# HGRN2 feature tile by feature tile from step 0.2 on, with TensorE's queue of the first stage in text order

## The chip, the cores and the metric

The kernel runs on one core of one Trainium2 chip, in one launch. The metric is the device time of one execution in microseconds (us). Five engines matter, each with a queue of its own that it works off from the front: TensorE for matmuls (PE in the profile; PEld is its weight load), VectorE (DVE), ScalarE (ACT), GpSimd (POOL) and SyncE (SP), which issues DMAs.

## What is computed

A decoder trunk of two layers over 1,024 positions and 1,024 features, in float32. Each layer projects the normed input once and splits the columns among four groups of 256 features: latent attention (A), forgetting attention (B), HGRN2 (C) and S5 (D). Their outputs go through an output projection into the residual, then come a gated MLP with a short convolution and a gated embedding. The change touches the groups C and D and the projection that feeds them:

```python
def hgrn2_group(q, f_logit, i_in, lb):              # group C, chunks of 64 positions
    ...
    def chunk_step(state, inp):
        q_c, k_c, v_c, lf_c = inp
        bcum = jnp.cumsum(lf_c, axis=2)
        decay = jnp.exp(jnp.where(causal[:, :, None], bcum[:, :, :, None, :] - bcum[:, :, None, :, :], -jnp.inf))
        scores = jnp.einsum('bhtk,bhsk,bhtsk->bhts', q_c, k_c, decay)
        o = jnp.einsum('bhts,bhsv->bhtv', scores, v_c) + jnp.einsum('bhtk,bhkv->bhtv', q_c * jnp.exp(bcum), state)
        ...                                          # the state goes on to the next chunk
def s5_group(u, ...):                                # group D: a complex diagonal scan, then
    zact = jax.nn.gelu(y)
    out = zact * jax.nn.sigmoid(zact @ w_glu + b_glu)
```

## The kernel before, in words

Tiles hold 128 features by 512 positions: a group of 256 features has two feature tiles (ft 0 and 1), the sequence two halves (n 0 and 1). A float32 product is three matmuls of rounded parts: pj (L738 to L740) for projections with features on partitions, 12 matmuls of 128x512 per weave step; ptk (L726 to L728) for those with positions on partitions.

The first stage of a layer is woven from generators by weave() (L683), which always advances the one with the lowest scheduled fraction, from the table T (L42):

- in_proj(), 68 steps from 0 to 1, the input projection: hq of ft 0 and the values v, then the mark "h0" (step 12, fraction 0.18); z and hq of ft 1, then "h1" (step 20, fraction 0.29); the misc tile, the attention's fq, fk and fv, HGRN2's output gates hg, and cq and ckv for attention A.
- s5(), from 0.1 to 0.7: for each ft its matrices and its core (sin L579; a chain of DVE instructions L585 to L609 on tiles s5z; ys L619 and L622; yf L635); then for all four tiles a GELU (L657 to L662, back and forth between ACT and DVE, to zh and zl), and the GLU: matmuls gl from zh and zl, and on ACT and DVE a sigmoid (L128 to L136, L676) for each of four gl tiles; then the norm (sq, ss L798, xn).
- hgrn(), 66 steps from 0.35 to 0.92: four units hgrn_unit, one for each (ft, n); a unit of n=1 takes over the state of n=0. A unit computes its gates (ACT and DVE, L217 to L237, to hk and hb), then kh (L267 to L269), transposes it on PE (khT, L292) and multiplies by v into pu (L301, the state); then comes a triangle of scores in seven levels: per level DVE L279, ACT L280 and L281, DVE L282 and twice L286 (qz), on PE four matmuls psc (L327), and on DVE L333 (into sc), each qz prepared one level ahead; at the end the diagonal (L337, L338) and poh (L351, L353).
- early(), in layer 0 only, from 0 to 0.2: constants.

Before, hgrn() waits for "h1", and then runs the units of both ft of n=0 in alternation, and after them those of n=1. The order in which each engine's queue holds this work is not that of the text: a scheduler of the framework orders all queues by its own estimates of durations and of what is ready. So a pj tile may stand ahead of a gl whose input comes late.

Around it: a first part of the projection (uf, z of ft 0) stands ahead of the weave; attention and the output projection (first instruction ob, L726), the MLP and the embedding follow.

Of the kernel before, what the change touches and what calls it, by code (L numbers as in the profile page):

```python
# [38 lines left out]

T = dict(early=(0, 0.2), s5=((0.1, 0.7), (0.1, 0.7)), hgrn=((0.35, 0.92), (0.35, 0.92)), cd=((0.05, 0.85), (0.05, 0.85)), prep=((0.3, 1), (0.3, 1)), b=(0, 1), a=(0.9, 0.95), pre=(7, 9, 11, 13), vals=(5, 6), ahead=3, plv=4, mx=0, pw=1, rt=2, sc=2, rp=6, dl=4, qk=(4, 4), up=5)  # L42


class Kern:
# [210 lines left out]
def hgrn_unit(K, layer, ft, n, z, q, v, lbc, st, y):  # L256
# [55 lines left out]
    for li in range(len(LEVELS) + 1):  # L312
        if li < len(LEVELS):
            g, qz = ahead
        if li == T['qk'][layer]:
            qk = K.h(name="qk")
# [42 lines left out]
HGRN_STEPS = 7 + len(LEVELS) + 1  # L359
# [283 lines left out]
S5_STEPS = 7 + 7  # L643
# [37 lines left out]
GLU_STEPS = 5  # L681


def weave(*gens):

    live = [[g, n, 0, span] for g, n, *span in gens]
    while live:
        e = min(live, key=lambda e: e[2] / e[1] if not e[3] else e[3][0] + (e[3][1] - e[3][0]) * e[2] / e[1])
        e[2] += 1
        try:  # L690
            next(e[0])
        except StopIteration:
            live.remove(e)
# [138 lines left out]
RMS_STEPS = 6  # L832
# [7 lines left out]
def proj(K, srcs, xs, evacs, m=P, banks=None, ws=None):  # L840

    ws = ws or [wload(K, s, len(xs) * m, hi_act=True, eng=K.nc.vector) for s in srcs]
    for n in range(2):
        for w, evac, bank in zip(ws, evacs, banks or [K.pd] * 3):
            ps = bank("pj")
            for _ in mm3_steps(K, ps[0:m, :], [(rows(*w, k, m), x[n]) for k, x in enumerate(xs)]):
                yield
            evac(n, ps[0:m, :])
            yield
# [19 lines left out]
class Head:  # L869
# [67 lines left out]

    def out(self, ahead=T['ahead']):

# [22 lines left out]
        for qh, kt in [(0, kt) for kt in range(4)] + [(1, kt) for kt in range(8)]:  # L962
# [11 lines left out]
            nc.scalar.activation(pr[:, 0:n], ps[:, 0:n], AF.Exp)  # L974
            K.lo(V if T['plv'] and kt % T['plv'] == T['plv'] - 1 else nc.gpsimd, pl[:, 0:n], pr[:, 0:n], ph[:, 0:n])
            pend.append((qh, kt, n, ph, pl))
# [8 lines left out]
def attention(heads):  # L985
# [13 lines left out]
    for i in range(len(heads)):  # L999
        nxt, pre = get(i + 2), iter(())  # L1000
        mx, vals = (b.max(), b.values()) if b else (iter(()), iter(()))
        for step, _ in enumerate(a.out()):
            for _ in range(2 if step % 2 or step < T['mx'] else 1):
                next(mx, None)
            if step == 6 and nxt:
# [3 lines left out]
                pre = nxt.prep()  # L1009
            if step in T['pre']:  # L1010
                next(pre, None)
            if step in T['vals']:
                next(vals, None)
# [9 lines left out]
def fox_cum(K, misc, bf):  # L1023


    nc = K.nc
    V = nc.vector
    r = slice(64, 68)
    prev = 0.0
    for n in range(2):  # L1030
        m, x, a = misc[n], K.h(name="fx"), K.h(name="fa")
        V.tensor_scalar(x[r], m[r], bf[r, 0:1], None, op0=ALU.add)
        nc.scalar.activation(a[r], x[r], AF.Abs)
        nc.scalar.activation(a[r], a[r], AF.Exp, scale=-1.0)
        nc.scalar.activation(a[r], a[r], AF.Ln, bias=1.0)
        V.scalar_tensor_tensor(x[r], x[r], 0.0, a[r], op0=ALU.min, op1=ALU.subtract)
        V.tensor_tensor_scan(a[r], K.ones[r, 0:1].to_broadcast([4, HS]), x[r], prev, op0=ALU.mult, op1=ALU.add)
        prev = a[r, HS - 1:HS]
        nc.gpsimd.memset(m[64:96, :], 0.0)
        nc.gpsimd.memset(m[96:102, :], 1.0)  # L1040
        V.tensor_scalar(m[r].bitcast(F32R), a[r], -1.0, None, op0=ALU.mult)
        V.scalar_tensor_tensor(m[96:100].bitcast(F32R), a[r], -1.0, m[r], op0=ALU.mult, op1=ALU.subtract)
# [409 lines left out]
def body(ctx, tc, xT, pT, pos, invf, sgn, vecs, prms, dsk, bfs, w_fm, w_misc, w_tm, w_uq, w_ukv, w_glu,  # L1452
         w_outb, w_up, w_down, w_pg, w_ple, out):
    nc = tc.nc
    K = Kern(tc, ctx)
# [45 lines left out]
    steps, lbc = [], K.const([P, 6], F32, "lbc")  # L1501
    ready = {}

    def early():

        for l in range(DEPTH):
            head = K.sm([P, 24], name="s5h", tag="s5h", bufs=2)
            nc.scalar.dma_start(head, prms[l][:, 0:24])
            steps.append(s5_steps(K, head))
            yield  # L1510
        rope_tables(K, pos, cst, tabs)
        K.exp_ln()
        hgrn_lb(K, vec[0][:, V_LB:V_LB + 4], lbc)
        ready["steps"] = True
        yield
        for _ in hgrn_consts(K):
            yield
        ready["consts"] = True
# [3 lines left out]
    for l in range(DEPTH):  # L1522
# [5 lines left out]
        z, hq, hv, hg, fq, fk, fv, misc, cq = ([] for _ in range(9))  # L1528

        def put(dst, name, m=P):  # L1530
            t = K.two(name=name)
            dst.append(t)
            return lambda n, ps: V.tensor_tensor(t[n][0:m, :], ps, r1[n], op=ALU.mult) if m == P else \
                V.tensor_tensor(t[n][0:m, :], ps, r1[n][0:m, :], op=ALU.mult)

        def fm(i, dst, name):
            return proj(K, [w_fm[l, i]], xs, [put(dst, name)])


        rt = K.sm([P, 8], name="rt", tag="rt", bufs=2)  # L1540

        def tokmaj(i, vt):
            def ev(gr, ps):
                t = K.h(name="v").rearrange("p (c f) -> p c f", f=256)
                vt.append(t)
                for j in range(2):
                    nc.scalar.activation(t[:, j, :], ps[:, j * 256:(j + 1) * 256], AF.Copy,
                                         scale=rt[:, 2 * gr + j:2 * gr + j + 1])

            return proj_tok(K, [w_tm[l, i, j] for j in range(2)], xs, ev)  # L1550
# [17 lines left out]
        def in_proj():  # L1568
            yield from fm(2, hq, "hq")
            yield from tokmaj(0, hv)  # L1570
            ready["h0"] = True
            yield from fm(1, z, "z")
            yield from fm(3, hq, "hq")
            ready["h1"] = True
            yield from proj(K, [w_misc[l]], xs, [put(misc, "misc", 68)], m=68)
            fox_cum(K, misc[0], bf)
            yield from fm(4, fq, "fq")
            yield from fm(6, fk, "fk")
            yield from tokmaj(2, fv)
            yield from fm(5, fq, "fq")  # L1580
            yield from fm(7, fk, "fk")
            for i in range(2):
                g = K.two(name="hg")

                def ev(n, ps):
                    t = K.h(name="sg")
                    V.tensor_tensor(g[n], ps, r1[n], op=ALU.mult)
                    K.sigmoid(g[n], g[n], t)

                yield from proj(K, [w_fm[l, 11 + i]], xs, [ev])  # L1590
                hg.append(g)
            ready["gates"] = True
            for i in range(2):
                yield from fm(8 + i, cq, "cq")
            yield from fm(10, cq, "ckv")

        IN_STEPS = 4 * 13 + 2 * 8
        yc, yd = [K.two(name="yc") for _ in range(2)], []
        yb, ya = ([K.two(name=n) for _ in range(2)] for n in ("yb", "ya"))
        h, ycs, yds, res, heads = [], [], [], {}, []  # L1600

        def s5():
            while "steps" not in ready:
                yield
            pr, yl = s5_params(K, prm, steps[l]), []
            for ft in range(2):
                r = {}
                yield from s5_mats(K, pr, ft, dk, r)
                yield from s5_core(K, r, uf[ft], yl)
            yield from s5_glu(K, yl, w_glu[l], vc[:, V_BGLU:V_BGLU + 2], yd)  # L1610
            yield from rms_steps(K, yd, gain(3), yds)

        def hgrn():
            st = [K.h(name="st") for _ in range(2)]
            while "h1" not in ready or "consts" not in ready:
                yield
            for n in range(2):
                u = [hgrn_unit(K, l, ft, n, z[ft][n], hq[ft][n], hv, lbc, st[ft], yc[ft]) for ft in range(2)]
                for _ in range(HGRN_STEPS):
                    for g in u:  # L1620
                        next(g, None)
                        yield
            while "gates" not in ready:
                yield
            yield from rms_steps(K, yc, gain(2), ycs, gates=hg)
# [17 lines left out]
            return get  # L1643

        pre = [(early(), 12, *T['early'])] if l == 0 else []
        weave(*pre, (s5(), 2 * S5_STEPS + GLU_STEPS + RMS_STEPS, *T['s5'][l]), (hgrn(), 4 * HGRN_STEPS + RMS_STEPS, *T['hgrn'][l]), (in_proj(), IN_STEPS, 0, 1))

        ready["fox"] = True

# [105 lines left out]
        xs, rp = nm.xs, nm.r  # L1755
# [6 lines left out]
        ws, pend, pw = {}, None, {}  # L1762
# [7 lines left out]
        for i, u in enumerate(units + [None]):  # L1770
# [3 lines left out]
            if pend:  # L1774
                n, m, c, v, t = pend
                V.scalar_tensor_tensor(t[:, c], v[:, c], 0.0, t[:, c], op0=ALU.min, op1=ALU.subtract)
                nc.scalar.activation(v[:, c], t[:, c], AF.Exp)
            if u:
                n, m, c = u
# [20 lines left out]
            if pend:  # L1800
                n, m, c, v, t = pend
# [101 lines left out]
```

## Time and profile before

| | us |
|---|---|
| median of 3 runs (lowest, highest) | 3041.83 (3039.55, 3045.96) |
| the profiled execution, its own time | 3032.95 |
| its span in the trace | 3031.2 |
| first stage, layer 0: from the first pk of S5 to the first ob | 88 to 425 |
| first stage, layer 1: the same | 1595 to 1906 |
| busy share of the span: PE, DVE, ACT, POOL | 93%, 73%, 47%, 35% |

The profile gives each instruction of each engine with its start and duration, and for a gap ahead of it the instruction that ended the gap. PEclk is the clock that TensorE was granted, as a share of its full 2.4 GHz: 1.00 is 2.4 GHz and 0.50 is 1.2 GHz. PE time in a window is the time in which some matmul was under way, so at the lower clock the same matmul counts for longer.

### The profile page before, as it was taken

The numbers are of one execution on the slowest core, as the hardware profiler recorded it, in microseconds if no ns is written. First come the engines' busy times: TensorE is split into PE (matmuls) and PEld (weight loads), VectorE is DVE, ScalarE is ACT, GpSimd is POOL, SyncE is SP. The second block draws the span as 40 slices with busy tenths as digits, with TensorE's granted clock in tenths as the row PEclk, the third lists the DMA queues.
The fourth block names the chain that finished last, engine by engine and source line by source line (L and its number), as shares of the span: only waits on it lengthen the run. The fifth ranks groups of instructions, "written<-read, shape, count | busy, mean of one in ns | idle before, by whom it ended". The sixth has DMA issues, their size and how long they took to land.

```text
span 3031.2 us, 37112 instructions
## 1 busy us (share of the span) xinstructions
PE 2825.1 (93%) x13346; PEld 2271.9 (75%) x13346; DVE 2208.3 (73%) x3254; ACT 1414.8 (47%) x2383; POOL 1068.9 (35%) x927
## 2 busy tenths in 40 slices
PE   7899799889899999999999888988989999999997
PEld 6777676666688888888787866766767888888886
DVE  6595768777999998242854966878699999953458
ACT  4234446665444444242732453657654444443346
POOL 2521013345422224555523210325453222255544
PEclk9898799899999999999999998999999999999998
DMA  3101011103222225352421010110032222263533
GB/s 125 38 15 49 22 59 35 35 1 132 70 83 84 84 84 172 130 191 92 152 88 36 19 56 28 53 56 1 31 123 90 82 82 82 82 212 98 185 107 129
DMA packets 112136, 249.68 MB, mean 82 GB/s; under 512 B 17488, under 2 KB 20176, under 8 KB 111952
## 3 DMA queue, kind: packets, MB, share of 16 engines
q1 hardware_dynamic: 110512, 246.66, 24.6%
q8 instruction: 105, 1.72, 0.2%
q10 hardware_dynamic: 1440, 0.65, 0.1%
q14 instruction: 79, 0.65, 0.1%
HBM read 197.58 MB, written 48.50 MB: 81 GB/s over the span
## 4 chain that ended last, share of the span: by engine, by line
PE 56%; DVE 21%; issue 7%; ACT 4%; POOL 2%; DMA 1%; SPq 0%; DVEq 0%; POOLq 0%; ACTq 0%
PE up L1320 8%; PE up L1319 8%; PE up L1318 8%; PE dn L1439 5%; PE dn L1440 5%; PE dn L1438 5%; DVE wx L103 1%; PE qk L968 1%; PE pj L738 1%; DVE mx L897 1%; DVE xq L1199 1%; PE pj L739 1%; PE ob L726 1%; PE pj L740 1%; PE ob L727 1%
## 5 line engine op out<-in xcount | busy, mean ns | idle before, releaser
L103 POOL TENSOR_TENSOR wx<-wr,wx 128x512 fp32r<-128x512 f32 (+1 forms) x293 | 485.6, 1670 | 362.2 <-ACT wx L1421 198.1
L1318 PE MATMUL up<-bh,wx 128*128 128x512 f32 x1232 | 482.8, 392 | 12.2 <-ACT wx L1311 12.2
L1319 PE MATMUL up<-bl,wx 128*128 128x512 f32 x1232 | 483.2, 392 | 7.0 <-DVE bl L103 4.0
L1320 PE MATMUL up<-bh,wx 128*128 128x512 f32 x1232 | 483.4, 392 | 6.3 <-DVE wx L103 6.3
L1318 PEld LDWEIGHTS up<-bh,wx 128*128 128x128 f32 x1232 | 233.5, 190 | 61.5 <-ACT wx L1311 13.1
L1439 PE MATMUL dn<-g,wx 128*128 128x512 f32 x704 | 274.1, 389 | 3.8 <-DVE g L103 3.8
L1319 PEld LDWEIGHTS up<-bl,wx 128*128 128x128 f32 x1232 | 233.5, 190 | 57.5 <-DVE bl L103 4.9
L1320 PEld LDWEIGHTS up<-bh,wx 128*128 128x128 f32 x1232 | 233.3, 189 | 56.9 <-DVE wx L103 8.3
L103 POOL TENSOR_TENSOR pl<-pr,ph 128x512 fp32r<-128x512 f32 x144 | 166.2, 1166 | 306.9 <-ACT pr L974 188.2
L1440 PE MATMUL dn<-g,wx 128*128 128x512 f32 x704 | 273.9, 389 | 0.0
L1438 PE MATMUL dn<-g,wx 128*128 128x512 f32 x704 | 273.9, 389 | 0.0
L103 DVE TENSOR_TENSOR g<-g,g 128x512 fp32r<-128x512 f32 x88 | 105.6, 1215 | 202.7 <-ACT g L1420 186.0
L103 POOL TENSOR_TENSOR wx<-wq,wx 128x512 fp32r<-128x512 f32 x44 | 65.1, 1479 | 517.5 <-ACT wx L1311 517.5
L738 PE MATMUL pj<-xs,wx 128*128 128x512 f32 (+1 forms) x512 | 212.3, 415 | 16.4 <-ACT xs L765 7.3
L1421 ACT CAST wx<-wr 128x1024 fp32r<-128x1024 f32 x88 | 92.4, 1050 | 277.9 <-PE dn L1439 255.4
L740 PE MATMUL pj<-xs,wx 128*128 128x512 f32 (+1 forms) x512 | 207.1, 405 | 2.5 <-DVE wx L103 2.5
L739 PE MATMUL pj<-xs,wx 128*128 128x512 f32 (+1 forms) x512 | 208.1, 406 | 1.1 <-DVE xs L766 1.1
L1439 PEld LDWEIGHTS dn<-g,wx 128*128 128x128 f32 x704 | 132.1, 188 | 32.1 <-DVE g L103 4.7
L1440 PEld LDWEIGHTS dn<-g,wx 128*128 128x128 f32 x704 | 132.1, 188 | 27.4
L1438 PEld LDWEIGHTS dn<-g,wx 128*128 128x128 f32 x704 | 132.1, 188 | 27.4
L1329 DVE SCALAR_TENSOR_TENSOR cv<-u,vec,cv 128x1023 f32<-128x1023 f32 x88 | 131.0, 1491 | 28.0 <-ACT cv L1328 27.8
L1330 DVE SCALAR_TENSOR_TENSOR cv<-u,vec,cv 128x1022 f32<-128x1022 f32 x88 | 137.8, 1568 | 0.1
(468 smaller groups left out, 6940.5 us busy)
## 6 DMA issues: line engine op xcount, KB each, us to landing
wr<-in_w_down SPq DMA_DIRECT2D x88, 512.0 KB, 3.5
wr<-in_w_up SPq DMA_DIRECT2D x88, 256.0 KB, 2.9
wq<-in_w_up SPq DMA_DIRECT2D x88, 256.0 KB, 3.9
hid<-cv SPq DMA_DIRECT2D x44, 512.0 KB, 3.3
g<-hid SPq DMA_DIRECT2D x88, 256.0 KB, 5.2
wr<-in_w_fm SPq DMA_DIRECT2D x30, 512.0 KB, 3.9
wr<-in_w_pg SPq DMA_DIRECT2D x28, 512.0 KB, 3.5
hdr<-h SPq DMA_DIRECT2D x48, 256.0 KB, 2.0
```

What stands on the lines that cost most here:

```text
L103: eng.tensor_tensor(out, x, hi.bitcast(F32), op=ALU.subtract)
L738: nc.tensor.matmul(out, lhsT=ah, rhs=bh, start=(i == 0), stop=False)
L739: nc.tensor.matmul(out, lhsT=ah, rhs=bl, start=False, stop=False)
L740: nc.tensor.matmul(out, lhsT=al, rhs=bh, start=False, stop=(i == n - 1))
L1318: nc.tensor.matmul(ps, lhsT=ah, rhs=bh, start=k == 0, stop=False)
L1319: nc.tensor.matmul(ps, lhsT=ah, rhs=bl, start=False, stop=False)
L1320: nc.tensor.matmul(ps, lhsT=al, rhs=bh, start=False, stop=k == KD // 2 - 1)
L1329: V.scalar_tensor_tensor(c[:, 1:], u[:, :S - 1], cw[:, 1:2], c[:, 1:], op0=ALU.mult, op1=ALU.add)
L1330: V.scalar_tensor_tensor(c[:, 2:], u[:, :S - 2], cw[:, 0:1], c[:, 2:], op0=ALU.mult, op1=ALU.add)
L1438: nc.tensor.matmul(ps[m], lhsT=ah, rhs=gh, start=f == 0, stop=False)
L1439: nc.tensor.matmul(ps[m], lhsT=ah, rhs=gl, start=False, stop=False)
L1440: nc.tensor.matmul(ps[m], lhsT=al, rhs=gh, start=False, stop=f == NFF - 1)
```

## The change

Three edits, for both layers. hgrn() starts at the fraction 0.2 and not at 0.35. It goes feature tile by feature tile: once "h0" is there, the units n=0 and n=1 of ft 0 run in alternation, and once "h1" is there, those of ft 1. And the weave of the first stage is put under a manual schedule for TensorE: PE's queue takes the order in which the generators issue, while the other queues are still ordered by the scheduler, around the new PE queue. Lines behind L1646 are one higher in the changed file.

```diff
-T = dict(..., hgrn=((0.35, 0.92), (0.35, 0.92)), ...)
+T = dict(..., hgrn=((0.2, 0.92), (0.2, 0.92)), ...)
...
             st = [K.h(name="st") for _ in range(2)]
-            while "h1" not in ready or "consts" not in ready:
-                yield
-            for n in range(2):
-                u = [hgrn_unit(K, l, ft, n, z[ft][n], hq[ft][n], hv, lbc, st[ft], yc[ft]) for ft in range(2)]
+            for ft in range(2):
+                while f"h{ft}" not in ready or "consts" not in ready:
+                    yield
+                u = [hgrn_unit(K, l, ft, n, z[ft][n], hq[ft][n], hv, lbc, st[ft], yc[ft]) for n in range(2)]
                 for _ in range(HGRN_STEPS):
...
-        weave(*pre, (s5(), 2 * S5_STEPS + GLU_STEPS + RMS_STEPS, *T['s5'][l]), (hgrn(), 4 * HGRN_STEPS + RMS_STEPS, *T['hgrn'][l]), (in_proj(), IN_STEPS, 0, 1))
+        with tc.manual_schedule(engines={mybir.EngineType.PE}):
+            weave(*pre, (s5(), 2 * S5_STEPS + GLU_STEPS + RMS_STEPS, *T['s5'][l]), (hgrn(), 4 * HGRN_STEPS + RMS_STEPS, *T['hgrn'][l]), (in_proj(), IN_STEPS, 0, 1))
```

No instruction is added or removed on any engine, apart from how a few neighbours are counted together. PE's queue is the same up to the first half of a pj tile ahead of S5's first ys in both layers, and again from the first ob on.

**Place 1, PE in layer 0.** Before, a whole pj tile (24 matmuls for hq) stands between the second half's sin and S5's first ys, and the first khT comes some 165 rows later. In the changed queue the first two khT stand in the middle of that pj tile:

```order
L740 MATMUL pj_1315<-xs_158,wx_1232 128x512
L292 MATMUL khT_1328<-ident,kh_1282 128x128 x4
L292 MATMUL khT_1343<-ident,kh_1309 128x128 x4
L738 MATMUL pj_1315<-xs_166,wx_1231 128x512
L739 MATMUL pj_1315<-xs_167,wx_1231 128x512
```

Their inputs are kh_1282 and kh_1309, the kh of the two halves of ft 0. On DVE these stand, in the changed queue, between and behind the steps of S5's chain for its first core:

```order
L267 TENSOR_TENSOR kh_1282<-hb_1145 128x512
L596 SCALAR_TENSOR_TENSOR s5z_1267<-dk_1277,s5z_1266 128x512
L1533 TENSOR_TENSOR hq_1227<-pj_1235,rs_260 128x512
L597 SCALAR_TENSOR_TENSOR s5z_1266<-dk_1277,s5z_1268 128x512
L269 TENSOR_TENSOR kh_1282<-kh_1282,hk_1144 128x512
L604 TENSOR_TENSOR s5z_1269<-s5z_1267,phr_1093 128x4x127
L606 TENSOR_TENSOR s5z_1270<-s5z_1266,phr_1093 128x4x127
L607 TENSOR_TENSOR s5z_1269<-s5z_1269,s5z_1268 128x4x127
L609 TENSOR_TENSOR s5z_1270<-s5z_1270,s5z_1267 128x4x127
L267 TENSOR_TENSOR kh_1309<-hb_1188 128x512
L279 TENSOR_TENSOR g_1335<-hb_1145 128x512
L269 TENSOR_TENSOR kh_1309<-kh_1309,hk_1187 128x512
```

What moved: HGRN2's first units into S5's chain on DVE, and their transposes to the place on PE where S5's chain has just begun.

**Place 2, PE in layer 0, the GLU.** Before, the matmuls for one zh tile stand alone, and 22 pj matmuls follow before the next zh is asked for:

```order
L353 MATMUL poh_2419<-qb_2213,st_1470 64x128
L726 MATMUL gl_2435<-zh_2241,wx_2382 128x512
L727 MATMUL gl_2435<-zl_2242,wx_2382 128x512
L728 MATMUL gl_2435<-zh_2241,wx_2383 128x512
L738 MATMUL pj_2493<-xs_114,wx_2489 128x512
L739 MATMUL pj_2493<-xs_114,wx_2489 128x512
```

In the changed queue the first two gl tiles, which take all four zh tiles, stand in a row right behind 96 ptk matmuls (and three rows of gl_2480 for zh_2315), and the first pj comes behind them:

```order
L726 MATMUL gl_2480<-zh_2378,wx_2443 128x512
L727 MATMUL gl_2480<-zl_2379,wx_2443 128x512
L728 MATMUL gl_2480<-zh_2378,wx_2444 128x512
L726 MATMUL gl_2497<-zh_2330,wx_2443 128x512
L727 MATMUL gl_2497<-zl_2331,wx_2443 128x512
L728 MATMUL gl_2497<-zh_2330,wx_2444 128x512
L726 MATMUL gl_2497<-zh_2393,wx_2443 128x512
L727 MATMUL gl_2497<-zl_2394,wx_2443 128x512
L728 MATMUL gl_2497<-zh_2393,wx_2444 128x512
L738 MATMUL pj_2528<-xs_114,wx_2524 128x512
```

The GELU makes zh_2315, zh_2330, zh_2378 and zh_2393 in this order. What moved: the pj work that stood between the gl groups is behind the first two of them.

**Place 3, DVE in layer 1, behind the GLU.** In the changed PE queue khT_14914 stands 24 pj matmuls behind the first two gl tiles (with the other two gl tiles amid these). Its input kh_14885 is finished by the last row here, behind the sigmoids of all four gl tiles; the gates of ft 1 (to hb_14596 and hb_14657) stand between the GELU and these:

```order
L237 SCALAR_TENSOR_TENSOR hb_14657<-anew,z_13344 128x512
L134 TENSOR_SCALAR gs_14858<-gl_14851,vec_65 128x512
L135 TENSOR_TENSOR gt_14859<-gs_14858,gt_14859 128x512
L676 TENSOR_TENSOR yd_14860<-yl_14560,gs_14858 128x512
L134 TENSOR_SCALAR gs_14875<-gl_14868,vec_65 128x512
L135 TENSOR_TENSOR gt_14876<-gs_14875,gt_14876 128x512
L676 TENSOR_TENSOR yd_14877<-yl_14561,gs_14875 128x512
L267 TENSOR_TENSOR kh_14885<-hb_14596 128x512
L1533 TENSOR_TENSOR fq_14830<-pj_14838,rs_12753 128x512
L267 TENSOR_TENSOR kh_14904<-hb_14657 128x512
L269 TENSOR_TENSOR kh_14885<-kh_14885,hk_14595 128x512
```

Before, the gates and kh of the units that come last stood behind the sigmoids too, but PE's queue had the first of their khT 111 rows behind the last gl, with pj matmuls for most of these.

## Rows read from the trace of the kernel before

**Rows 1.** Busy time by window, both first stages: us, busy (instructions) per engine, PEclk, DMA

```profile
88.00:425.00 337.00, 297.91 (x1586) 236.62 (x1585) 224.63 (x462) 123.69 (x242) 72.27 (x105) 0.86 0.13 40
1595.00:1906.00 311.00, 277.93 (x1587) 222.50 (x1587) 220.69 (x416) 125.43 (x245) 59.72 (x80) 0.93 0.13 42
```

**Rows 2.** Windows at PEclk 0.50, layer 0: the longest of nine, and their sum

```profile
359.40:386.70 27.30, 18.66 (x70) 15.64 (x70) 19.17 (x31) 9.84 (x20) 2.50 (x2) 0.50 0.00 1
sum 95.50, PE 83.85 PEld 63.62 DVE 46.31 ACT 31.50 POOL 17.37; mean PE 9.32 PEld 7.07 DVE 5.15 ACT 3.50 POOL 1.93
```

**Rows 3.** The same for layer 1: the first of four, and their sum

```profile
1632.60:1646.30 13.70, 13.70 (x43) 9.84 (x44) 0.07 (x1) 1.29 (x4) 9.02 (x23) 0.50 0.11 40
sum 44.10, PE 36.42 PEld 28.93 DVE 19.76 ACT 13.94 POOL 9.02; mean PE 9.10 PEld 7.23 DVE 4.94 ACT 3.49 POOL 2.26
```

**Rows 4.** Waits of PE, layer 0, 80 to 420: us in total, times, longest

```profile
PE psc L327 <- DVE qz L286: 14.8, 8, 3.1
PE khT L292 <- DVE kh L269: 6.1, 2, 3.3
PE gl L726 <- DVE zh L662: 3.5, 1, 3.5
```

**Rows 5.** Waits of PE, layer 1, 1560 to 1920

```profile
PE psc L327 <- DVE qz L286: 18.1, 9, 3.2
```

**Rows 6.** Timeline of PE, last levels of a unit: start, us, instructions [idle before]

```profile
371.67 2.05 PE L327 MATMUL psc<-qz,g 128*128 128x128 f32 x8 [2.51 <-DVE qz L286]
376.23 2.05 PE L327 MATMUL psc<-qz,g 128*128 128x128 f32 x8 [2.51 <-DVE qz L286]
```

**Rows 7.** Timeline of PE, layer 0, to S5's first ys

```profile
128.18 0.39 PE L738 MATMUL pj<-xs,wx 128*128 128x512 f32 x1
128.41 0.39 PE L739 MATMUL pj<-xs,wx 128*128 128x512 f32 x1
...
129.54 0.38 PE L619 MATMUL ys<-tz,ut 128*128 128x128 f32 x2
131.91 0.48 PE L622 MATMUL ys<-care,s5z 64*128 64x128 f32 x2 [1.99 <-DVE s5z L607]
```

**Rows 8.** Timeline of DVE, layer 0, S5's first chain and behind it

```profile
118.34 1.76 DVE L103 TENSOR_TENSOR wx<-wr,wx 128x1024 fp32r<-128x1024 f32 x1 [1.80 <-ACT wx L714]
120.56 0.69 DVE L585 TENSOR_TENSOR s5z<-sin,phr 128x512 f32<-128x512 f32 x1 [0.47 <-PE sin L579]
...
127.84 0.66 DVE L604 TENSOR_TENSOR s5z<-s5z,phr 128x508 f32<-128x508 f32 x1
...
132.38 0.68 DVE L1533 TENSOR_TENSOR hq<-pj,rs 128x512 f32<-128x512 f32 x1
...
153.15 0.69 DVE L1534 TENSOR_TENSOR misc<-pj,rs 68x512 f32<-68x512 f32 x1 [18.96 <-PE pj L740]
```

**Rows 9.** Timeline of PE, layer 0, ptk

```profile
237.26 0.28 PE L726 MATMUL ptk<-wx,xs 128*128 128x256 f32 x1
237.38 0.28 PE L727 MATMUL ptk<-wx,xs 128*128 128x256 f32 x1
```

**Rows 10.** Timeline of ACT, layer 0, the GELU's tiles

```profile
254.22 0.63 ACT L657 ACTIVATE ga<-yl 128x512 f32<-128x512 f32 x1
...
263.24 0.63 ACT L657 ACTIVATE ga<-yl 128x512 f32<-128x512 f32 x1
...
270.00 0.61 ACT L657 ACTIVATE ga<-yl 128x512 f32<-128x512 f32 x1
```

**Rows 11.** Timeline of DVE, layer 0, the last zh

```profile
277.58 0.43 DVE L662 CAST zh<-yl 128x512 fp32r<-128x512 f32 x1
```

**Rows 12.** Timeline of DVE, layer 1: the GLU's last two tiles, then a gate's last two steps

```profile
1785.60 0.69 DVE L676 TENSOR_TENSOR yd<-yl,gs 128x512 f32<-128x512 f32 x1 [0.70 <-ACT gs L136]
...
1788.89 0.69 DVE L676 TENSOR_TENSOR yd<-yl,gs 128x512 f32<-128x512 f32 x1 [0.70 <-ACT gs L136]
...
1804.38 0.67 DVE L235 SCALAR_TENSOR_TENSOR z<-z,ha 128x512 f32<-128x512 f32 x1
...
1805.60 1.23 DVE L237 TENSOR_TENSOR_SCAN hb<-anew,z 128x512 f32<-128x512 f32 x1
```

More of the change, by code (lines that the diff above doesn't have):

```diff
@@ L37 @@
 NS5 = 24 + 4 * 128
-T = dict(early=(0, 0.2), s5=((0.1, 0.7), (0.1, 0.7)), hgrn=((0.35, 0.92), (0.35, 0.92)), cd=((0.05, 0.85), (0.05, 0.85)), prep=((0.3, 1), (0.3, 1)), b=(0, 1), a=(0.9, 0.95), pre=(7, 9, 11, 13), vals=(5, 6), ahead=3, plv=4, mx=0, pw=1, rt=2, sc=2, rp=6, dl=4, qk=(4, 4), up=5)
+T = dict(early=(0, 0.2), s5=((0.1, 0.7), (0.1, 0.7)), hgrn=((0.2, 0.92), (0.2, 0.92)), cd=((0.05, 0.85), (0.05, 0.85)), prep=((0.3, 1), (0.3, 1)), b=(0, 1), a=(0.9, 0.95), pre=(7, 9, 11, 13), vals=(5, 6), ahead=3, plv=4, mx=0, pw=1, rt=2, sc=2, rp=6, dl=4, qk=(4, 4), up=5)
 class Kern:
```

## The prediction

> **What bounds the kernel now.** I read the windows of the two first stages first, since no instruction outside them changes place on PE. PE is busy for 297.9 of 337 us in layer 0 and 277.9 of 311 us in layer 1, DVE for some 220 us in each [rows 1]: PE sets the end, and DVE has room on the whole, but not everywhere. Next come the windows in which PE's granted clock is 0.50, which is its lower level of 1.2 GHz: nine in layer 0 with 83.9 us of PE's work, four in layer 1 with 36.4 us [rows 2, 3]. At the full clock that work would take half, so the lower clock costs 42 and 18 us. So a stage has three parts: work at full clock (297.9 - 42 = 256 us, and 277.9 - 18 = 260 us), the excess of the lower clock (42 and 18 us), and PE's idle time (337 - 298 = 39 us, and 311 - 278 = 33 us). The change adds no work, and so it acts on the last two alone: 81 us in layer 0 and 51 us in layer 1, 132 us together.
>
> Then the waits. The largest is HGRN2's: psc waits for qz for 14.8 us in layer 0 and 18.1 us in layer 1 [rows 4, 5]. Where psc groups stand in a row, two units' levels come every 4.56 us and PE idles for 2.51 us in each such pair, at the lower clock [rows 2, 6]. Against that, DVE stands idle for 18.96 us ahead of misc in layer 0, while PE runs ys and pj [rows 8]. An earlier HGRN2 could use that.
>
> **What the change takes away.** In the new PE queue a step of 12 pj matmuls stands between one or two psc groups nearly everywhere. A pj follows the one before in 0.23 us [rows 7], so such a step is 2.7 us, while a level of one unit takes DVE about 4.56 / 2 = 2.3 us [rows 6]. So most of the psc waits go: 15 and 18 us, of which I leave 4 us per layer. DVE's idle time ahead of misc shrinks too. That is worth nothing by itself, since it is not PE's.
>
> **What it adds: PE in text order stands behind results that come late.** A PE queue in text order has no pj to run while its head waits. I went through it place by place.
>
> *The first khT, layer 0.* PE comes to khT 12 pj (2.7 us) ahead of where ys starts now, at 129.54 - 2.7 = 126.8 [rows 7]. Now the steps of S5's chain up to L604 take DVE until 127.84 [rows 8]. Ahead of kh_1282 the new queue puts six more short steps (0.67 us each) and two scans (1.23 us each) [rows 12], 6.5 us, of which waits of 1.80 and 0.47 us that DVE has there now [rows 8] cover 2.3 us. So it is ready at 127.8 + 6.5 - 2.3 = 132, a wait of 5 us. Then kh_1309 stands behind the rest of the chain (now 127.84 to 132.38, 4.5 us [rows 8]) and three short steps, so 6.5 us later: 6 us more for the next khT. The 2 us that ys waits now [rows 7] is gone. In layer 1 the same transposes come later than S5's chain, and I take 3 us for them. A second core's ys there waits for its chain, 6 us.
>
> *The GLU.* The GELU takes its four tiles one after the other through ACT and DVE: 6.8 us from one start to the next where nothing else comes between, 9.0 us where casts of weights do, and 8.0 us from a tile's start to the end of its zh (270.00 to 278.0) [rows 10, 11]. The first gl tile now needs zh tiles one and three, and the second all four. The third zh comes some 1 + 6.8 + 9.0 + 8.0 = 25 us behind yf, plus a little for gates on ACT; PE has 96 ptk of 0.12 us between [rows 9], 11.8 us. It waits for 14 us, then 6 us more for the fourth. Before, PE filled this with pj and waited for 3.5 us [rows 4]. In layer 1, where 16 poh come in addition, 12 and 6 us.
>
> *Behind the GLU.* A sigmoid of a gl tile takes 3.3 us [rows 12]. In layer 1, behind the fourth zh, DVE's queue holds ft 1's gates (ten short steps, a scan, a cast, 9 us), two sigmoids, a scan, two more sigmoids (14.4 us) and four short steps (2.6 us) before kh_14885 is done: 26 us. PE has gl and 24 pj until khT_14914, 9 to 10 us, and waits for 16 us. In layer 0 the kh of the first half stands ahead of the sigmoids, and the second's behind two of them: 15 us against 10, a wait of 5 us. S5's norm (ss) follows, its input sq behind further qz steps: by the same count 7 and 6 us in layer 0, and 6 us in layer 1.
>
> Idle time of PE is then, in layer 0, 5 + 6 + 14 + 6 + 5 + 7 + 6 + 4 = 53 us (now 39), and in layer 1, 3 + 6 + 12 + 6 + 16 + 6 + 4 = 53 us (now 33).
>
> **The clock.** The lower clock now comes in stretches that cost 42 / 9 = 4.7 us each in layer 0 and 18 / 4 = 4.6 us in layer 1 [rows 2, 3], and the first in layer 1 is all PE work, 13.7 us, behind a wait in ys. The long waits above are six in layer 0 if neighbours count once, so 28 us instead of 42; the row of psc groups at the lower clock for 27.3 us [rows 2] goes. In layer 1 I leave 18 us: its long stretch falls away and the waits at gl and khT bring as much. The Trainium skill ("TensorE: Matmul & The Clock Gate", Part 1) says of the ramp to the full clock that for modeling it is under 1% of a typical kernel's span, which would be under 30 us here; the rows of this trace have 60 us, 2% of the span, in the two stages alone, so the measurement decides and the clock stays in my sum. With no change in the clock the sum would be the idle time's alone, the third rival below.
>
> **Sum.** Layer 0: 256 + 53 + 28 = 337 us, against 337 now: 0. Layer 1: 260 + 53 + 18 = 331 us, against 311: +20. Together +20 us on the profiled execution of 3032.95 us, which lies 9 us under the median of 3041.83; on the median, **3062 us**. Bounds: if every wait above is half of what I count (the 98 us without the 4 us left per layer become 49), the sum is 49 us lower, -29. If the waits stand and each brings a stretch like the longest of those now (27.3 us with 18.7 us of work, 9.3 us lost [rows 2]) in two places per layer instead of 4.7 us, it is 18 us higher, +38.
>
> **The rivals.**
>
> *The load spreads well (faster).* The units start in DVE's empty time, text order mixes pj and psc evenly, and DVE and ACT, relieved of the crowd at the end, deliver the GELU, kh and sq sooner than I count. It decides at 132 us: if idle time and clock excess of both layers stay under that, the kernel gains. With the GLU's waits as counted (38 us), the other waits halved (60 to 30 us), 8 us of small ones and three stretches per layer at the lower clock (28 us) they are 104 us: -28, **3014 us**. For it: DVE's 18.96 us of idle time [rows 8], and 33 us of psc waits that go [rows 4, 5]. Against it: the GELU is a serial chain that no spreading shortens, and nothing in PE's new queue covers it.
>
> *Gain and loss cancel (no change).* If waits at the end go and new ones in the middle come in equal measure, the time is 3042 us. For it: in layer 0 my own sum is 0. Against it: layer 1 has less lower clock to win.
>
> *The clock does not recover (slower still).* The waits move but stretches at the lower clock keep their 60 us: the idle time alone counts, 106 - 72 = +34, **3076 us**. For it: now too a wait of 2 us stands ahead of 13.7 us at the lower clock [rows 3, 7].
>
> **How the numbers follow.** My forecast has a chance of 0.45, between 3047 and 3082 by itself; the clock rival 0.10; no change 0.13; the spreading rival 0.32, since every wait that I add rests on counting DVE's queue. About 6 us (0.2%) is what a measurement of this kernel can tell from no change. So faster 0.32, same 0.13, slower 0.55. The range from 3006 to 3088 us takes in both bounds and the better part of the spreading rival.
>
> **What would show it.** Right, if PE's waits show gl behind zh with 10 us and more in one wait in each layer, khT behind kh with over 10 us in layer 0's first pair and in layer 1 behind the GLU, and psc behind qz with little. The first stage of layer 0 should be about as long as before, that of layer 1 longer by some 20 us. Wrong, if the gl waits are under 5 us, or PEclk stays at 1.00 through the later half of both stages and the idle time of the two layers is under 85 us.

## The result, and the profile after

The changed kernel takes 3076.88 us (median of 4 runs, 3071.59 to 3079.15) against 3040.69 us before on the same chips (3037.76 to 3045.96): a ratio of 1.0121, interval 1.0108 to 1.0134, or 36 us more. The profiled executions stand 44.6 us apart (spans of 3075.8 and 3031.2 us). Of these, layer 0's first stage has 7.6 us (337.1 to 344.7 us) and layer 1's 38.6 us (310.8 to 349.4 us); all else together is 1.6 us shorter. The busy time by window of the two stages, which answers to [rows 1] (window, length, then busy time of PE, PEld, DVE, ACT, POOL, PEclk, DMA share, GB/s):

```profile
87.90:432.60 344.70, 279.01 (x1585) 223.79 (x1585) 229.28 (x461) 130.08 (x250) 76.00 (x105) 0.88 0.12 39
1601.30:1950.70 349.40, 294.42 (x1586) 235.79 (x1586) 221.78 (x419) 135.18 (x259) 63.07 (x84) 0.85 0.12 38
```

The sums of the windows at PEclk 0.50, seven in layer 0 and nine in layer 1, which answer to [rows 2, 3]:

```profile
sum 81.80, PE 44.01 PEld 32.88 DVE 60.88 ACT 31.22 POOL 13.98; mean PE 6.29 PEld 4.70 DVE 8.70 ACT 4.46 POOL 2.00
sum 102.40, PE 77.45 PEld 60.11 DVE 60.79 ACT 31.66 POOL 15.53; mean PE 8.61 PEld 6.68 DVE 6.75 ACT 3.52 POOL 1.73
```

By the prediction's three parts: the work at full clock is 279.0 - 22.0 = 257 us in layer 0 and 294.4 - 38.7 = 256 us in layer 1 (before 256 and 260). The lower clock costs 22 us in layer 0 (before 42) and 39 us in layer 1 (before 18). PE's idle time is 65.7 us and 55.0 us (before 39 and 33). The waits of PE of the changed kernel, layer 0 (us in total, times, longest):

```profile
PE khT L292 <- DVE kh L269: 17.2, 3, 6.2
PE gl L726 <- DVE zh L662: 14.6, 2, 12.0
PE psc L327 <- DVE sc L333: 11.2, 1, 11.2
PE ss L798 <- DVE sq L790: 9.2, 3, 6.0
```

And of layer 1:

```profile
PE khT L292 <- DVE kh L269: 16.0, 1, 16.0
PE gl L726 <- DVE zh L662: 13.1, 2, 10.5
PE ys L622 <- DVE s5z L607: 6.7, 2, 5.2
PE ss L798 <- DVE sq L790: 6.1, 2, 3.8
...
PE psc L327 <- DVE qz L286: 0.4, 1, 0.4
```

The waits for qz [rows 4, 5] are gone, and the waits that the prediction named are there, most of them near the sizes it gave. One it did not name: 11.2 us at psc in layer 0. By the profile it ends with sc (L333), the step of DVE that reads the psc before. On DVE, the timeline of that stretch shows what stands ahead of it: the forget gate's sums of attention B (L1032 to L1042 on fx and misc), which the queue holds between two levels of HGRN2. The next qz comes late behind the same steps (its second half is the row at 191.12), and the last row is the sc that ends the wait:

```profile
178.16 0.48 DVE L1032 TENSOR_SCALAR fx<-misc,bf 4x512 f32<-4x512 f32 x1
...
184.35 2.27 DVE L1037 TENSOR_TENSOR_SCAN fa<-ones,fx 4x512 f32<-4x512 f32 x1
...
191.12 0.48 DVE L286 SCALAR_TENSOR_TENSOR qz<-g,heads,hq 128x256 f32<-128x256 f32 x1
...
192.72 0.69 DVE L333 COPY_PREDICATED sc<-lm,psc 128x512 f32<-128x512 uint8 x1
```

And VectorE's own longest waits, one piece in each layer (layer 0, then layer 1):

```profile
DVE ga L658 <- ACT ga L657: 30.1, 2, 28.8
```
```profile
DVE ga L658 <- ACT ga L657: 33.2, 2, 31.9
```

Here DVE stands still for 29 and 32 us ahead of the GELU's first step, while PE works off poh, ys and ptk. That becomes the question of the experiments: is the loss PE's waits, or the time that DVE lost before them?

### The profile page after: what moved, and what is told of

Its sections match the earlier page's. It is cut to its first block, busy times and chain, and to the rows that moved or that the text cites. A ratio compares the mean times of both kernels' runs of the same rounds, so it can differ in the third digit from the quotient of the medians.

```text
span 3075.8 us, 37103 instructions
## 1 busy us (share of the span) xinstructions
PE 2823.4 (92%) x13346; PEld 2274.6 (74%) x13346; DVE 2211.3 (72%) x3254; ACT 1416.8 (46%) x2383; POOL 1073.4 (35%) x927
## 4 chain that ended last, share of the span: by engine, by line
PE 60%; DVE 24%; issue 7%; ACT 5%; POOL 2%; DMA 1%; SPq 0%; DVEq 0%; ACTq 0%; POOLq 0%
PE up L1320 8%; PE up L1319 8%; PE up L1318 8%; PE dn L1439 5%; PE dn L1440 5%; PE dn L1438 5%; PE pj L738 2%; PE pj L739 2%; PE pj L740 2%; DVE wx L103 2%; PE qk L968 1%; DVE xq L1199 1%; DVE mx L897 1%; PE ob L726 1%; DVE h L1807 1%
## 5 line engine op out<-in xcount | busy, mean ns | idle before, releaser
L1318 PEld LDWEIGHTS up<-bh,wx 128*128 128x128 f32 x1232 | 233.8, 190 | 61.6 <-ACT wx L1311 13.1
L738 PE MATMUL pj<-xs,wx 128*128 128x512 f32 (+1 forms) x512 | 222.5, 435 | 9.0 <-ACT xs L765 7.1
L739 PE MATMUL pj<-xs,wx 128*128 128x512 f32 (+1 forms) x512 | 210.4, 411 | 0.6 <-DVE xs L766 0.6
L740 PE MATMUL pj<-xs,wx 128*128 128x512 f32 (+1 forms) x512 | 209.7, 410 | 0.9 <-DVE wx L103 0.9
```

The source lines that it names most:

```text
L738: nc.tensor.matmul(out, lhsT=ah, rhs=bh, start=(i == 0), stop=False)
L739: nc.tensor.matmul(out, lhsT=ah, rhs=bl, start=False, stop=False)
L740: nc.tensor.matmul(out, lhsT=al, rhs=bh, start=False, stop=(i == n - 1))
L1318: nc.tensor.matmul(ps, lhsT=ah, rhs=bh, start=k == 0, stop=False)
```

## The experiments

Ratios are to the kernel before, run beside each one; 1% is 30 us.

### Which of the three edits

Text order alone (`e_man`): the changed kernel with HGRN2 as before.

```diff
-hgrn=((0.2, 0.92), (0.2, 0.92))
+hgrn=((0.35, 0.92), (0.35, 0.92))
-            for ft in range(2):
-                while f"h{ft}" not in ready or "consts" not in ready:
-                    yield
-                u = [hgrn_unit(K, l, ft, n, ...) for n in range(2)]
+            while "h1" not in ready or "consts" not in ready:
+                yield
+            for n in range(2):
+                u = [hgrn_unit(K, l, ft, n, ...) for ft in range(2)]
```

> Only the third edit: TensorE's queue of the first stage in text order, HGRN2 as before (both feature tiles in alternation, from 0.35). Theory 1 (a queue in text order stands behind late results, whatever HGRN2's order): the gl tiles stand in a row behind the GELU here too, so waits at gl of 10 to 20 us in each layer, and a time 20 to 45 us above the kernel before (3060 to 3085). Theory 2 (the loss comes from HGRN2's early start inside S5's chain, in VectorE's queue): about the time of before, 3030 to 3050, since HGRN2's units start after S5's first chain here.

Measured: 3073.01 us, 1.0119 (1.0102 to 1.0136). The first two edits without the third (`e_ftstart`):

```diff
-        with tc.manual_schedule(engines={mybir.EngineType.PE}):
-            weave(...)
+        weave(...)
```

> The first two edits without the third: HGRN2 by feature tile from 0.2 on, all queues ordered by the scheduler. Theory 1 (text order on TensorE is what costs): pj matmuls stand between the gl tiles again, no wait of TensorE over 6 us, and a time within 12 us of before (3029 to 3053). Theory 2 (the early start and the order by feature tile cost): 20 us and more above before (3060 and up), with waits at khT.

Measured: 3016.92 us, 0.9934 (0.9917 to 0.9950): faster than theory 1 gave, and with a wait of PE over 6 us after all (in layer 1 it waits 10.4 us at pj for fq).

Once more, for a narrower interval (`e_ftstart2`):

> The first two edits without text order on TensorE once more, beside the other run on the same chip, for a narrower interval: 0.990 to 0.996 of before.

Measured: 3018.24 us, 0.9941 (0.9926 to 0.9955).

By feature tile in text order, but from 0.35 on (`e_ftman`, the first line of the first diff here alone):

> The second and third edit, with HGRN2 from 0.35 on as before: by feature tile, TensorE in text order. Theory 1 (waits at the GLU and behind it): the first pair of khT in layer 0 no longer waits behind S5's first chain, -11 us of idle time there, but gl waits as in the changed kernel (12 and 10 us) and HGRN2 ends later, so 3060 to 3085. Theory 2 (the start at 0.2 is what costs): back to within 12 us of before.

Measured: 3074.01 us, 1.0124 (1.0108 to 1.0141): the time of theory 1, though not by its waits (gl waits 6.2 us in layer 0, khT 14.9 us at a later place). By feature tile alone (`e_ft`), and the start alone (`e_start`), both with the scheduler's queues:

> The second edit alone: HGRN2 by feature tile, from 0.35 on, all queues ordered by the scheduler. With the first two edits together the time fell by 0.66% (some 20 us). Theory A (the early start brings the gain, since it fills VectorE's empty time): within 6 us of before. Theory B (the order by feature tile brings it, since the second tile's gates no longer come in one crowd): 10 to 20 us under before.

> The first edit alone: HGRN2 from 0.2 on, both feature tiles in alternation, which still waits for h1 (step 20 of 68 of the projection, fraction 0.29), all queues ordered by the scheduler. Theory A (the start brings the gain): 8 to 20 us under before. Theory B (only with the order by feature tile can it start early): within 8 us of before.

Measured: `e_ft` 3037.94 us, 0.9999 (0.9973 to 1.0025); `e_start` 3030.76 us, 0.9984 (0.9974 to 0.9993), 5 us under before. So theory A's figure holds for `e_ft` and theory B's for `e_start`: neither edit alone brings the gain.

| HGRN2 | scheduler's PE queue | PE queue in text order |
|---|---|---|
| as before | 1 | 1.0119 |
| by feature tile, from 0.35 | 0.9999 | 1.0124 |
| alternating, from 0.2 | 0.9984 | not run |
| by feature tile, from 0.2 | 0.9934, 0.9941 | 1.0121 (the change) |

In the three settings that were run, text order ends at 1.012: it costs 1.2% in two of them and 1.8% in the third, where it also takes back the gain of 0.6% that the other two edits have together (the start alone has 0.16%, the order by feature tile alone none). So the third edit is the one that costs: theory 1 of these runs holds in that, and theory 2 falls. Not so theory 1's detail: with HGRN2 as before and in text order, PE waits at gl for 3.7 us at the longest, not for 10 to 20 us. The third edit also leaves the other engines' queues to be ordered anew around PE's, and no run separates that from PE's own order. The waits of PE in `e_man`, layer 0, then layer 1:

```profile
PE khT L292 <- DVE kh L269: 15.5, 2, 8.1
PE psc L327 <- DVE qz L286: 10.1, 5, 5.3
PE ss L798 <- DVE sq L790: 8.0, 3, 3.3
PE gl L726 <- DVE zh L662: 6.3, 2, 3.7
```
```profile
PE psc L327 <- DVE qz L286: 15.2, 6, 6.8
PE ss L798 <- DVE sq L790: 13.0, 3, 8.0
PE khT L292 <- DVE s5t L394: 8.5, 1, 8.5
PE gl L726 <- DVE zh L662: 4.4, 2, 3.1
```

The stages are as long as in the change, but the waits lie elsewhere. No one place makes the loss. The two stages of `e_man`:

```profile
89.60:435.30 345.70, 295.69 (x1586) 234.31 (x1586) 227.89 (x461) 129.66 (x250) 71.37 (x105) 0.85 0.12 39
1604.50:1951.50 347.00, 294.97 (x1586) 234.42 (x1586) 224.91 (x419) 135.54 (x259) 62.99 (x84) 0.86 0.12 38
```

And of `e_ftstart`:

```profile
90.00:411.60 321.60, 276.93 (x1585) 219.40 (x1585) 229.23 (x461) 127.28 (x246) 77.54 (x105) 0.92 0.13 42
1580.70:1894.80 314.10, 279.25 (x1586) 223.60 (x1586) 219.81 (x419) 131.56 (x255) 63.16 (x84) 0.91 0.13 42
```

PE is idle for 44.7 and 34.9 us here, against 65.7 and 55.0 us in the change, and its busy time is 2 and 15 us less for the same work. These four differences, 58 us, account for the 57.9 us between the two spans (3017.9 and 3075.8 us): 41 us of idle time and 17 us of busy time, which for the same work is the lower clock. Between `e_man` and the kernel before it is 30 us of idle time (102 against 72) and 15 us of busy time. So text order mostly adds idle time, and some lower clock with it.

The gain of 0.6% is of the other kind. Against the kernel before, PE is not less idle in `e_ftstart` (80 us in the two stages, before 72); its busy time is 20 us less, at a granted clock of 0.92 and 0.91 (before 0.86 and 0.93).

The start matters: HGRN2 by feature tile from 0.27 with the scheduler's queues (`s27`).

```diff
-hgrn=((0.2, 0.92), (0.2, 0.92))
+hgrn=((0.27, 0.92), (0.27, 0.92))
```

> By feature tile, all queues ordered by the scheduler, but HGRN2 from 0.27 and not from 0.2 on. With 0.2 the two edits gave 20 us (0.66%), with 0.35 nothing. Theory B (the order by feature tile lets HGRN2 run in the 19 us that VectorE stands idle ahead of misc): at 0.27 HGRN2's first units come about when misc does, so half or less of the gain: 4 to 12 us under before. Rival (any start between does): 16 to 24 us under before.

Measured: 3040.64 us, 1.0003 (0.9991 to 1.0015): no gain at all, less than either theory gave. DVE's wait ahead of misc in layer 0, 19.0 us before [rows 8], is still there at 0.27, and the view of DVE's waits of `e_ftstart` in that layer lists none of 2 us or more there:

```profile
DVE misc L1534 <- PE pj L740: 14.3, 1, 14.3
```

That fits the idea that filling this gap is where the 0.6% comes from, but no run filled it by other work alone. What the two runs do show is the clock. In layer 0, PE's busy time is 299.4 us at 0.27 and 276.9 us at 0.2, with a granted clock of 0.84 and 0.92:

```profile
89.40:429.90 340.50, 299.35 (x1586) 237.73 (x1586) 224.60 (x460) 125.90 (x246) 74.73 (x105) 0.84 0.12 40
```

### Is it the wait at gl?

Four empty steps of S5 ahead of the first gl in the changed kernel, so that other work comes first (`a_glu`):

```diff
     wh, wl = wload(K, w, 512, hi_act=True, eng=V)
     yield
+    for _ in range(4):
+        yield
     for m in range(2):
...
-GLU_STEPS = 5
+GLU_STEPS = 9
```

> The changed kernel with four empty weave steps of S5 ahead of the first gl, so that in text order some four steps of the projection (2.7 us each) and HGRN2's levels come before it. Theory 1 (TensorE's wait at gl is itself what costs): the gl waits, 12.0 + 2.6 us in layer 0 and 10.5 + 2.6 us in layer 1, fall to under 5 us per layer, and the time is 15 to 30 us under the changed kernel, that is 6 to 21 us above before. Rival (VectorE is late by so much that the wait only moves on): khT, ss or psc wait for what gl no longer does, and the time stays within 8 us of the changed kernel, 28 to 44 us above before.

Measured: 3081.62 us, 1.0153 (1.0133 to 1.0172). The wait at gl fell to 2.5 us in layer 0 and is no longer listed in layer 1, and the time did not fall. By the time the rival holds: others are there instead (PE's waits, layer 0, then layer 1):

```profile
PE khT L292 <- DVE kh L269: 15.8, 2, 9.1
PE ss L800 <- DVE sq L792: 14.7, 3, 6.3
PE utp L567 <- ACT uc L560: 7.6, 1, 7.6
```
```profile
PE poh L351 <- ACT yc L355: 15.5, 1, 15.5
PE ys L622 <- DVE s5z L607: 14.2, 2, 11.0
```

The edit does more than delay gl, though. weave() spreads S5's steps over the same stretch of fractions, now 43 steps and not 39, so all its earlier steps come sooner in the text too. The waits at utp and ys lie ahead of gl (in layer 0 they end at 204 and 235 us, and gl comes at 290 us): they did not take the place of the wait at gl, they come from S5's earlier steps. So the run does not price the wait at gl alone.

Extra matmuls in place of the idle time (`a_fill`); they write into the gl tile, which the real ones then start afresh:

```diff
             ps = K.px("gl")
+            for _ in range((44, 9)[n] if m == 0 else 0):
+                nc.tensor.matmul(ps, lhsT=wh[:, 0:P], rhs=xs[0][n][0], start=True, stop=True)
             mm3(K, ps, ...)
```

> The changed kernel with 44 extra matmuls of 128x512 (0.23 us each, 10 us) ahead of the first gl and 9 ahead of the second, in both layers, on a zh tile that is ready: they take the place of idle time, and the real matmuls follow with a fresh start. Theory 1 (a wait costs twice: its idle time, and the lower clock that follows it): PEclk stays at 1.00 where the changed kernel shows 0.50 for 20 us around gl in each layer, and the time is 8 to 20 us under the changed kernel although work is added. Rival (the lower clock there comes from the short matmuls, or costs nothing since VectorE is late anyway): within 5 us of the changed kernel or above it.

Measured: 3077.59 us, 1.0129 (1.0110 to 1.0147), the time of the changed kernel. The clock did in part what theory 1 said. The windows around gl, first the changed kernel's (layers 0 and 1), then those of `a_fill`, with the stretch right behind in layer 1 and the one ahead of khT:

```profile
277.40:297.80 20.40, 8.31 (x17) 5.46 (x18) 13.37 (x18) 9.84 (x19) 4.14 (x3) 0.50 0.13 43
1792.90:1813.40 20.50, 10.04 (x21) 6.78 (x22) 12.07 (x18) 10.69 (x18) 3.48 (x3) 0.50 0.06 22
```
```profile
277.40:291.00 13.60, 10.56 (x47) 8.18 (x45) 8.43 (x12) 8.94 (x16) 2.60 (x2) 1.00 0.26 77
1796.50:1810.00 13.50, 10.33 (x42) 7.43 (x40) 7.35 (x12) 6.11 (x11) 2.47 (x3) 1.00 0.11 38
1810.00:1816.90 6.90, 5.75 (x14) 4.49 (x15) 4.52 (x7) 4.68 (x8) 1.09 (x1) 0.51 0.00 0
1827.20:1844.30 17.10, 5.52 (x15) 4.56 (x16) 12.34 (x20) 9.16 (x17) 0.00 (x0) 0.50 0.01 1
```

While the 44 extra matmuls run, PEclk is 1.00 where it was 0.50. But in layer 1 it falls to 0.51 right behind them, where the first pj behind gl stand, and PE is ready for khT 217.6 us after the stage's first pk, against 217.9 us. So there the clock that was kept up bought next to nothing. In layer 1 the wait at khT is 16.0 us again:

```profile
PE khT L292 <- DVE kh L269: 16.0, 1, 16.0
```

Some 10 us of work were put into the wait at gl in each layer, and the stages stayed 345.9 and 349.1 us long: PE has that time to spare, and what ends the waits comes from DVE and ACT. In layer 1, the step that completes kh starts 29.1 us behind the fourth zh in both runs. What a clock that stays up behind gl too would be worth, the run does not tell.

### The time that VectorE lost

The GELU of S5's first two tiles moved in the text to behind their own core (`g_man`), in the changed kernel:

```diff
             for ft in range(2):
                 r = {}
                 yield from s5_mats(K, pr, ft, dk, r)
                 yield from s5_core(K, r, uf[ft], yl)
-            yield from s5_glu(K, yl, ...)
+                yield from s5_gelu(K, yl[ft], xg)
+            yield from s5_glu(K, yl, xg, ...)
```

> The changed kernel with the GELU of S5's first two tiles moved in the text to right behind their own core, so that it no longer stands on ScalarE behind the copies of the second core. In the changed kernel VectorE waits for the GELU's first step for 28.8 us in layer 0 and 31.9 us in layer 1, in one piece. Theory 3 (VectorE's late half, not TensorE's wait itself, sets the end: the 30 us that it stands idle ahead of the GELU are missing behind it): that wait falls by half or more, the first gl wait to under 5 us, khT and ss behind the GLU wait less, and the time is 15 to 35 us under the changed kernel, 1 to 21 us above before. Rival (as with the four empty steps, another wait takes the place): within 8 us of the changed kernel, 28 to 44 us above before.

Measured: 3062.93 us, 1.0076 (1.0048 to 1.0103), 14 us under the changed kernel. DVE's waits ahead of the GELU, layer 0 and layer 1, then PE's largest in layer 0 and the one at gl:

```profile
DVE ga L656 <- ACT ga L655: 23.6, 1, 23.6
```
```profile
DVE ga L656 <- ACT ga L655: 24.0, 1, 24.0
```
```profile
PE psc L327 <- DVE qz L286: 21.1, 3, 8.9
...
PE gl L730 <- DVE zh L660: 5.5, 2, 2.9
```

DVE's wait fell by 5 and 8 us, not by half, and the time by about as much as both together: just short of what theory 3 gave, and more than the rival. Of the edits that left PE in text order, it is the only one that moved the time down. The price is new: PE waits for qz again, 21.1 us in layer 0. But theory 3's account is not shown by it. The two stages, and the second pass of ys in layer 1:

```profile
90.50:430.30 339.80, 278.07 (x1586) 223.50 (x1586) 230.93 (x460) 130.55 (x250) 75.25 (x105) 0.90 0.13 40
1605.10:1942.00 336.90, 280.55 (x1585) 225.98 (x1585) 225.06 (x419) 135.69 (x259) 64.88 (x84) 0.89 0.12 39
1764.10:1773.70 9.60, 9.60 (x57) 7.15 (x56) 0.00 (x0) 2.13 (x6) 0.00 (x0) 1.00 0.00 0
```

PE is idle for 61.7 and 56.4 us, in sum only 3 us less than in the changed kernel. What fell is its busy time, by 14 us in layer 1, at a granted clock of 0.89 against 0.85. The second pass of ys takes 9.6 us at 1.00; in the changed kernel it takes from 1739.5 to 1756.4 us, with waits of 1.9 us in it, and from 1741.7 us on the clock is 0.50. DVE waits for the GELU behind that pass, so the 8 us by which its wait fell in layer 1 can come from the clock as well. That is a rival to theory 3, and no run separates the two.

The same move with the scheduler's PE queue (`g_ftstart`):

> The first two edits without text order on TensorE (20 us under before), with the same earlier GELU. There VectorE waits for the GELU's first step for 15.4 us in layer 0 and 17.9 us in layer 1. Theory 3: that time is used, 5 to 15 us more, so 25 to 35 us under before, the fastest kernel so far. Rival (with a scheduler's queue TensorE has other work there, so nothing waits for it): within 5 us of the kernel without the move, 15 to 25 us under before.

Measured: 3019.51 us, 0.9936 (0.9910 to 0.9961), as without it: there the rival holds. The fastest of all is the change without its third edit, with this move or without.

## Why the prediction was right, and where not

The time, 3077, lies in the range and on the forecast's side. Of the signs that the prediction named, the waits came true; the stage lengths did not: layer 0 was to stay as it was and is 7.6 us longer, layer 1 was to be some 20 us longer and is 38.6 us. Step by step:

- **The waits that go.** psc behind qz: 33 us of waits, of which I left 8; the trace has 0.4 us in layer 1 and lists none in layer 0. Right as to qz; but psc still waits, 11.2 us in layer 0 and 5.9 us in layer 1 for sc and g.
- **The first khT in layer 0**: 5 and 6 us forecast, 5.5 and 5.4 us measured, and the third 6.2 us against 5. Right.
- **The GLU**: 14 + 6 us forecast in layer 0 and 12 + 6 us in layer 1, 12.0 + 2.6 us and 10.5 + 2.6 us measured. The third tile within 2 us, the fourth too high. Its zh comes 6.6 us behind the third one's (casts at 284.81 and 291.37 in layer 0), near the 6.8 us that I took. But I took nearly all of that as a wait, and PE spends 4.0 us of it on the six gl matmuls between, at the lower clock, and on a wait for zl.
- **khT behind the GLU in layer 1**: 16 us forecast, 16.0 us measured. ss: 13 and 6 us forecast, 9.2 and 6.1 us measured.
- **Idle time**: 53 and 53 us forecast, 65.7 and 55.0 us measured. The waits that I named came to 41.0 and 41.9 us, where I had 49 in each layer; the others to 24.7 and 13.1 us, where I had 4. That layer 1's sum is right within 2 us is luck. The largest that was missing is the wait of 11.2 us at psc in layer 0. I followed DVE's queue at the places where PE's head had changed, and not where the forget gate's sums had come to stand between two levels.
- **The clock** is the term that was mis-sized. For layer 0 I had 28 us and it was 22. "In layer 1 I leave 18 us" failed: it was 39 us, and that step alone is 21 us of the distance from +20 us to the +44.6 us of the profile. The waits at gl and khT brought 8 us of it, near what I meant for them; "its long stretch falls away" is what was wrong. I tied the stretches to long waits; but two of the longest in layer 1 are nearly all work, the first of them at the place of that long stretch:

```profile
1639.30:1659.80 20.50, 20.00 (x61) 14.41 (x62) 10.61 (x16) 3.96 (x10) 8.47 (x19) 0.50 0.09 27
...
1741.70:1762.20 20.50, 20.10 (x74) 16.16 (x74) 4.41 (x5) 1.29 (x4) 0.00 (x0) 0.50 0.08 26
```

These are mostly the two passes of ys, behind waits of 5.2 and 1.5 us. The clock as a whole costs 61 us in the two stages, as it did before (60): it moved from layer 0 to layer 1. So the sum of the third rival, with the clock's cost unchanged (3076 us), is nearest to the time measured, by way of an idle time that came to 121 us where it had 106. That it is so near is in part luck: the profiled executions stand 44.6 us apart, the medians 36 us. The Trainium skill's figure ("TensorE: Matmul & The Clock Gate", Part 1), under 1% of a typical kernel's span, is for the ramp to the full clock; it does not stand for this kernel's sixteen stretches at the lower clock, which cost 61 us, 2.0% of 3075.8 us.

- **The cause.** The account by work, idle time and clock is right as an account, and that the third edit is what costs is shown. But I read each wait of PE as a cost of its own. `e_man` speaks against it: other waits, and the same time; and in `a_fill` the wait at gl took 10 us of extra work at no cost in time. That what is lost is the time in which DVE and ACT stand still while PE works through a long piece of text is argued, not shown: `g_man` gained 14 us, but mostly in PE's clock. The 1.2% is spread over many waits, and no run singles them out.
- **The rival that the load spreads well** was priced at 3014 us. The first two edits do that without the third: 3016.92 and 3018.24 us. Its sum has 76 us of idle time and 28 us for the clock; `e_ftstart` has 80 us, and 40 us if the work at full clock is still 516 us. So the gain is in the clock there, as in that sum. But the rival was priced for PE in text order, and with it the gain did not come. My argument against it, "nothing in PE's new queue covers it", held for the change: its longest wait at gl is 12.0 us, against 1.9 us in `e_ftstart` (both in layer 0).

## What to carry to other kernels

Text order on one engine did not pay here, where the text had not been written with the lateness of every input in mind; the scheduler's queue, which can put a ready projection tile ahead of a late operand, was worth 1.2%, and 1.8% once the work could start early. Try the parts of such a change one at a time and together: two edits that did nothing (0.9999) or little (0.9984) alone gave 0.6% together, and the third hid it. Before a wait is costed, ask what the engine that ends it was waiting for earlier: if the wait can be filled with free work at no cost, it is not the engine that waits that sets the end there. And split every gain and loss into idle time and busy time: here two gains that looked like filled gaps were mostly a higher clock.

## What was not expected of the hardware

The granted clock fell to 0.50 for 20 us in windows in which PE was busy for 20.0 and 20.1 of 20.5 us by the profile, most of it small matmuls of ys (128x128 and 64x128). In `g_man` the same pass of ys runs at 1.00, busy for 9.6 of 9.6 us; what decides between the two levels no run here shows. And with 44 matmuls of 128x512, 10.2 us of work that nobody needs, it stood at 1.00 around gl, without any effect on the time. One open point is `e_start`: its first stages end 19 and 12 us earlier than before (406.2 and 1893.6 us), but the first matmul of the MLP only 4 us earlier in layer 0 (746.6 against 750.9 us) and 3 us later in layer 1; how the attention stage gives the gain back was not followed. Its profiled execution, 3036.1 us, is also the slowest of its ten, so its trace does not show where its 0.16% comes from.
